# PEER's routing steps spread over the rows of experts up to row 63, with seven tenths of the weights' second parts on GpSimd meanwhile

## The chip, the cores and the metric

One core of a Trainium2 chip runs the whole program. The metric is device microseconds of one execution. The kernel before took 2245.97, 2244.51 and 2240.70 us in three runs: the median is 2244.51.

## The reference

Two blocks run one after the other on 256 tokens of width 1024 (16 meta tokens ahead of them). The first block has a mixer (a state-space model beside a convolution) and a PEER layer; the second has two layers of attention between SwiGLU layers. The change is in PEER. Cut to what matters, in float32:

```
q  = x @ w_query                      # 256 tokens, 8 heads, two halves of 128
s1 = q1 . sub_keys_1 ; s2 = q2 . sub_keys_2        # 128 scores each
v1, i1 = top_k(s1, 16) ; v2, i2 = top_k(s2, 16)
cand = v1[:, None] + v2[None, :]                   # 16 x 16 per head
top_s, pos = top_k(cand, 16)
expert = i1 * 128 + i2 at pos ; gate = softmax(top_s)
y = sum over the chosen experts of gate * gelu(x . w_down[expert]) * w_up[expert]
```

There are 16384 experts (128 x 128), and each token uses 128 of them (16 in each of 8 heads).

## The kernel before, in words

**All experts are computed.** The kernel does not gather. It multiplies all tokens with all experts' down weights, row by row: a row is 128 experts (the first index fixed), and there are 128 rows. The GELU of a row's 128 x 256 products goes to `buf[:, row]`. A dense map of gates (expert by token, zero for experts that are not chosen) is then multiplied into it, and a second pass over all rows (the up projection, line 999) sums the results over experts in four PSUM banks.

**Weights in two parts.** A float32 product is made of three matmuls of the type fp32r: first part x first part, first x second, second x first. SyncE loads weights in chunks of eight tiles (512 KB, three buffers); `_split` (line 283) turns half a chunk (four tiles) into a first part wH on ScalarE (line 288) and a second part wL = weight - wH (line 294). The second part is made by VectorE or GpSimd: `self.turn` grows by `self.share` for each half chunk, and where it reaches 1, GpSimd takes this one. `wtile` (line 299) keeps up to four half chunks split ahead. A row of experts has eight weight tiles: 24 matmuls of 256 columns, and two second parts. `self.share` is 0.7 in the query stage (left from the mixer), 0.5 in the rows and 0.0 from the up projection on.

**The stages of `peer` (line 796).** First the queries (line 845): 16 tiles of q, each evacuated by VectorE to `buf[:, 100 + m % 4]` (lines 834, 835), multiplied with the keys (rows 104 to 111) one tile later (line 840), and the scores copied to rows 112 to 127 (line 841). Then the 128 rows of the down projection (loop at line 964). While they run, VectorE does the routing in two generators, `route(0)` and `route(1)` (line 869), one for each half of the tokens. A route has 40 steps: 16 top-16 lists over 128 scores (lines 863 to 867: MAX8, FIND_INDEX8, MATCH_REPLACE8, MAX8, FIND_INDEX8), sums of candidates (line 881), eight lists over 54 candidates, for eight heads an equality with an iota, a product and a reduction over 16 x 54 elements (lines 894, 895, 897), a softmax with its Exp on ScalarE (line 901), index arithmetic (lines 909 to 914), and three PE transposes with copies to `sel` and `gsel` (lines 918 to 922). The loop takes 1.5 steps after each row.

**Where the routing's scratch lies.** The scratch is in rows of `buf` that are not yet written: `hot` (16 x 54 per head) in rows 72 to 98, `small` from row 60 on. `carve` cuts `small` into v (256 values, one row), ii (one row), fi (one row), cand, cidx and smaller ones, some eight rows in all. The tile framework finds which instructions touch the same bytes and makes the later one wait.

**Gates.** From row 60 on (line 975) each row brings one group of four tokens: `onehot` (line 928) makes one-hot vectors of the two halves of the index on VectorE (line 931) and scales one by the gates (line 933, or line 936 on ScalarE); one row later `gates` (line 938) multiplies them on PE (line 943) to the 128 x 128 gate map of each token, VectorE multiplies it into the rows that are done (line 945), and ScalarE copies the rest into the rows that are to come (line 947). For those `value` (line 954) multiplies GELU and gates (lines 957 to 961), on GpSimd in odd rows. The first gates stand at row 61, the last (of 64) at row 124. After row 127, `act` (line 988) splits `buf[:, 0]` for the up projection.

**Order.** The framework lays out the order of each engine's queue when the program is built, by the source's order and by what is ready; the engines then run their queues in order.

```
    at += n                                   # carve: small[:, at : at + n]
    v = carve(8, 2, 16)
    ii = carve(8, 2, 16)
    q = buf[:, 100 + m % 4]                   # qf
```

Of the kernel before, what the change touches and what calls it, by code (L numbers as in the profile page):

```python
# [21 lines left out]
S = 256  # L22
# [185 lines left out]
class Net:  # L208
# [587 lines left out]
    def peer(self):  # L796
# [4 lines left out]
        NT = P  # L801
        with ExitStack() as ctx:
# [6 lines left out]
            rows = lambda a, b: buf[:, a:b].rearrange("p a b -> p (a b)")  # L809
# [1 line left out]
            keys = rows(104, 112).rearrange("p (h w k) -> p h w k", w=2, k=P)  # L811
            nc.scalar.dma_start(out=keys, in_=self.I["keys"])
            hot = rows(72, 99)[:, : 128 * 54].rearrange("p (h j c) -> p h j c", j=16, c=54)
            small = rows(60, 72)
            at = 0

            def carve(*shape):
# [110 lines left out]
            def onehot(g):  # L928
                o = oh[g % 2]
                ts = slice(4 * g, 4 * g + 4)  # L930
                nc.vector.tensor_tensor(out=o, in0=self.iota[:, None, None, :].to_broadcast([P, 4, 2, P]), in1=sel[:, ts, :, None].to_broadcast([P, 4, 2, P]), op=ALU.is_equal)  # L931
                if g % 4 == 0:
                    nc.vector.tensor_tensor(out=o[:, :, 0], in0=o[:, :, 0], in1=gsel[:, ts, None].to_broadcast([P, 4, P]), op=ALU.mult)
                else:
                    for t in range(4):
                        nc.scalar.activation(out=o[:, t, 0], in_=o[:, t, 0], func=AF.Copy, scale=gsel[:, 4 * g + t : 4 * g + t + 1])  # L936

            def gates(g, R):

                o = oh[g % 2]  # L940
                ps = self.bank("acc").rearrange("p (i t) -> p i t", t=4)
                for t in range(4):
                    nc.tensor.matmul(ps[:, :, t], o[:, t, 1], o[:, t, 0], start=True, stop=True)  # L943
                ts = slice(4 * g, 4 * g + 4)
                nc.vector.tensor_tensor(out=buf[:, :R, ts], in0=ps[:, :R], in1=buf[:, :R, ts], op=ALU.mult)
                if R < NT:
                    nc.scalar.activation(out=buf[:, R:, ts], in_=ps[:, R:], func=AF.Copy)

            pace = 0.0
            work = [x for tt in range(2) for x in [route(tt)]]  # L950
# [3 lines left out]
            def value(r, ps):  # L954
                n = 4 * done
                if n < S:
                    nc.scalar.activation(out=buf[:, r, n:], in_=ps[:, n:], func=AF.Gelu)
                if n:
                    t = self.t_("t", 2)
                    nc.scalar.activation(out=t[:, :n], in_=ps[:, :n], func=AF.Gelu)  # L960
                    (nc.gpsimd if r % 2 else nc.vector).tensor_tensor(out=buf[:, r, :n], in0=t[:, :n], in1=buf[:, r, :n], op=ALU.mult)

            self.share = 0.5
            for r_ in range(NT):
                self.linear(1, KD, self.u(M, T), S, lambda m, ps: value(r_, ps))
                pace += 1.5
                while pace >= 1:
                    pace -= 1
                    while work:
                        try:  # L970
                            next(work[0])
                            break
                        except StopIteration:
                            work.pop(0)
                if r_ >= 60:
                    assert not work
                    if pend >= 0 and done < S // 4:
                        gates(pend, r_ + 1)
                        done += 1
                    if pend + 1 < S // 4:  # L980
                        pend += 1
                        onehot(pend)
# [604 lines left out]
```

## Time and profile before

| | |
|---|---|
| median of three runs | 2244.51 us (2240.70 to 2245.97) |
| the profiled execution's own time | 2239.97 us |
| its span in the profile | 2238.0 us |
| busy: TensorE, VectorE, ScalarE, GpSimd | 2169.0, 1590.4, 1323.0, 671.7 us |
| mean granted TensorE clock | 0.995 |
| second parts on VectorE and on GpSimd (line 294) | 1037 of 731 ns, 259 of 1485 ns |

Times in the views are microseconds from the start of the span, or nanoseconds where marked. In a window view each engine has its busy time and, in brackets, its number of instructions; in a timeline a line has start, length, engine, source line, operation, output and inputs, a count where several stand together, and in square brackets the idle time before it and who ended it. PE is TensorE's matmuls, PEld its weight loads, DVE VectorE, ACT ScalarE, POOL GpSimd, SP SyncE. Matmuls overlap in the records (each shows 280 ns, one begins every 118), so their rate is read from counts.

### The profile page before, as it was taken

The page shows a single profiled execution, that of the slowest core. Times are in us where ns is not written, and L with a number is a line of the kernel's source. Part 1 is how long each engine was busy: PE and PEld are TensorE (multiplying, and loading weights), DVE is VectorE, ACT ScalarE, POOL GpSimd, SP SyncE. Part 2 cuts the span into 40 slices and gives each one's busy share as a digit, 9 for nine tenths or more (in the row PEclk, how much of TensorE's full clock was granted, in tenths as well). Part 3 has the DMA queues.
Part 4 walks back from the last instruction along what each step waited for, and adds up shares of the span by engine and source line. Part 5 has one row for each costly group of instructions (what it writes and reads, how often), then busy time and mean ns, then how long its engine had stood idle before and what let it go on. Part 6 is the DMA issues. An engine that isn't in the chain of part 4 may idle for free.

```text
span 2238.0 us, 45779 instructions
## 1 busy us (share of the span) xinstructions
PE 2169.0 (97%) x17351; PEld 2096.4 (94%) x17351; DVE 1590.4 (71%) x3143; ACT 1323.0 (59%) x2857; POOL 671.7 (30%) x567
## 2 busy tenths in 40 slices
PE   8998998899999999999999999999999999899999
PEld 7987998899999999999999998899999999679999
DVE  8889789955778766666586655876656666877664
ACT  8776654556766755555565555765555555666553
POOL 6684744444555400000031114122201211512220
PEclk9999999999999999999999999999999999999999
DMA  4523644454444555555565554145555555204555
GB/s 170 166 97 133 201 148 142 154 186 151 142 136 139 181 189 188 186 184 188 186 207 188 179 168 144 58 150 173 178 179 170 177 174 187 76 29 128 192 183 169
DMA packets 103948, 356.59 MB, mean 159 GB/s; under 512 B 12416, under 2 KB 20016, under 8 KB 103344
## 3 DMA queue, kind: packets, MB, share of 16 engines
q1 hardware_dynamic: 100096, 346.06, 46.8%
q10 hardware_dynamic: 3632, 7.62, 1.1%
q8 instruction: 136, 2.23, 0.4%
q14 instruction: 84, 0.69, 0.1%
HBM read 351.51 MB, written 5.40 MB: 159 GB/s over the span
## 4 chain that ended last, share of the span: by engine, by line
PE 76%; DVE 14%; ACT 5%; issue 3%; POOL 1%; DMA 1%; DVEq 0%; SPq 0%; ACTq 0%; POOLq 0%
PE acc L999 16%; PE mm L317 13%; PE mm L315 13%; PE mm L316 13%; PE acc L317 4%; PE acc L315 4%; PE acc L316 4%; DVE wL L294 3%; DVE h L931 2%; ACT h L936 1%; ACT wH L288 1%; DVE acc L526 1%; PE mm L1461 1%; PE acc L1485 1%; PE acc L943 1%
## 5 line engine op out<-in xcount | busy, mean ns | idle before, releaser
L288 ACT ACTIVATE wH<-raw 128x512 fp32r<-128x512 f32 x1296 | 806.6, 628 | 559.9 <-PE mm L316 237.8
L294 DVE TENSOR_TENSOR wL<-raw,wH 128x512 fp32r<-128x512 f32 x1037 | 756.3, 731 | 381.0 <-ACT wH L288 358.7
L317 PE MATMUL mm<-uH,wL 128*128 128x256 f32 (+1 forms) x2168 | 620.1, 286 | 19.9 <-DVE wL L294 19.2
L315 PE MATMUL mm<-uH,wH 128*128 128x256 f32 (+1 forms) x2168 | 628.3, 290 | 9.9 <-ACT wH L288 7.0
L316 PE MATMUL mm<-uL,wH 128*128 128x256 f32 (+1 forms) x2168 | 618.9, 286 | 2.4 <-DVE uL L359 2.3
L294 POOL TENSOR_TENSOR wL<-raw,wH 128x512 fp32r<-128x512 f32 x259 | 383.4, 1485 | 462.9 <-ACT wH L288 354.0
L317 PEld LDWEIGHTS mm<-uH,wL 128*128 128x128 f32 x2168 | 411.0, 190 | 24.7 <-DVE wL L294 23.8
L315 PEld LDWEIGHTS mm<-uH,wH 128*128 128x128 f32 x2168 | 410.9, 190 | 15.5 <-ACT wH L288 8.7
L316 PEld LDWEIGHTS mm<-uL,wH 128*128 128x128 f32 x2168 | 410.7, 189 | 5.9 <-DVE uL L359 4.2
L999 PE MATMUL acc<-uH,wH 128*128 128x256 f32 x1024 | 288.4, 282 | 1.7 <-DVE h L1033 1.1
L999 PE MATMUL acc<-uL,wH 128*128 128x256 f32 x1024 | 287.7, 281 | 0.4 <-DVE uL L357 0.4
L999 PE MATMUL acc<-uH,wL 128*128 128x256 f32 x1024 | 287.2, 281 | 0.0
L1086 POOL TENSOR_TENSOR t<-t,g 128x272 f32<-128x272 f32 (+1 forms) x88 | 108.2, 1231 | 415.6 <-ACT wH L288 326.2
L317 PE MATMUL acc<-uH,wL 128*128 128x272 f32 (+1 forms) x728 | 209.4, 288 | 0.0
L315 PE MATMUL acc<-uH,wH 128*128 128x272 f32 (+1 forms) x728 | 209.1, 287 | 0.0
L316 PE MATMUL acc<-uL,wH 128*128 128x272 f32 (+1 forms) x728 | 208.7, 287 | 0.0
L317 PE MATMUL mm<-gH,wL 128*128 128x272 f32 (+1 forms) x704 | 199.9, 284 | 0.0
L315 PE MATMUL mm<-gH,wH 128*128 128x272 f32 (+1 forms) x704 | 199.9, 284 | 0.0
L316 PE MATMUL mm<-gL,wH 128*128 128x272 f32 (+1 forms) x704 | 199.8, 284 | 0.0
L999 PEld LDWEIGHTS acc<-uH,wH 128*128 128x128 f32 x1024 | 194.1, 190 | 2.5 <-DVE h L1033 1.5
L999 PEld LDWEIGHTS acc<-uL,wH 128*128 128x128 f32 x1024 | 193.1, 189 | 0.6 <-DVE uL L357 0.6
L999 PEld LDWEIGHTS acc<-uH,wL 128*128 128x128 f32 x1024 | 193.0, 189 | 0.0
(400 smaller groups left out, 3918.0 us busy)
## 6 DMA issues: line engine op xcount, KB each, us to landing
raw<-in_wall_dram SPq DMA_DIRECT2D x648, 512.0 KB, 3.3
bdram<-brow ACTq DMA_DIRECT2D x1, 3200.0 KB, 13.7
b<-bdram SPq DMA_DIRECT2D x8, 272.0 KB, 4.6
b<-bdram SPq DMA_DIRECT2D x8, 144.0 KB, 4.2
buf<-in_keys_dram ACTq DMA_DIRECT2D x1, 1024.0 KB, 6.4
hd<-h ACTq DMA_DIRECT2D x1, 1024.0 KB, 5.4
h<-hd ACTq DMA_DIRECT2D x1, 1024.0 KB, 6.4
uv<-in_uv_dram ACTq DMA_DIRECT2D x1, 1024.0 KB, 5.8
```

The source lines that it names most:

```text
L288: nc.scalar.activation(out=H, in_=w, func=AF.Copy)
L294: eng.tensor_tensor(out=L, in0=w, in1=H.bitcast(F32), op=ALU.subtract)
L315: mm(ps, H, xH, start=(k == 0), stop=False)
L316: mm(ps, H, xL, start=False, stop=False)
L317: mm(ps, L, xH, start=False, stop=(k == kt - 1))
L526: nc.vector.scalar_tensor_tensor(out=acc, in0=src, scalar=w, in1=acc, op0=ALU.mult, op1=ALU.add)
L931: nc.vector.tensor_tensor(out=o, in0=self.iota[:, None, None, :].to_broadcast([P, 4, 2, P]), in1=sel[:, ts, :, None].to_broadcast([P, 4, 2 ...
L936: nc.scalar.activation(out=o[:, t, 0], in_=o[:, t, 0], func=AF.Copy, scale=gsel[:, 4 * g + t : 4 * g + t + 1])
L943: nc.tensor.matmul(ps[:, :, t], o[:, t, 1], o[:, t, 0], start=True, stop=True)
L999: nc.tensor.matmul(o, a, b, start=(r == 0 and d % 2 == 0 and i == 0), stop=(r == NT - 1 and i == 2), skip_group_check=True)
L1086: nc.gpsimd.tensor_tensor(out=t, in0=t, in1=s, op=ALU.mult)
L1461: nc.tensor.matmul(ps[:, :nk], qa[hh][:, k, a : a + n], ckv[:, k, :nk], start=(k == 0), stop=(k == 1))
```

## The change

The scratch `small` moves from rows 60 to 71 to rows 99 to 110. The gates begin at row 63 (128 - 64 - 1) instead of 60, so that the last of the 64 groups stands at row 127. The routing takes 80 / 62 = 1.29 steps a row instead of 1.5, and is spread over the rows up to the gates. While there is routing left, `self.share` is 0.7 instead of 0.5.

```diff
-            small = rows(60, 72)
+            small = rows(99, 111)
...
-            self.share = 0.5
+            first = NT - S // 4 - 1
             for r_ in range(NT):
+                self.share = 0.7 if work else 0.5
                 self.linear(1, KD, self.u(M, T), S, lambda m, ps: value(r_, ps))
-                pace += 1.5
+                pace += 80 / (first - 1)
                 while pace >= 1:
                     pace -= 1
                     while work:
...
-                if r_ >= 60:
+                if r_ >= first:
                     assert not work
                     if pend >= 0 and done < S // 4:
                         gates(pend, r_ + 1)
```

## Rows read from the trace of the kernel before

**Rows 1.** The page, part 1: busy time, share of the span and instructions.

```profile
PE 2169.0 (97%) x17351; PEld 2096.4 (94%) x17351; DVE 1590.4 (71%) x3143; ACT 1323.0 (59%) x2857; POOL 671.7 (30%) x567
```

**Rows 2.** Windows: length, PE, PEld, DVE, ACT, POOL busy, clock, DMA share, GB/s.

```profile
316.35:374.60 58.25, 51.62 (x401) 50.39 (x402) 58.18 (x147) 29.63 (x57) 24.19 (x16) 0.94 0.42 140
374.60:403.10 28.50, 22.45 (x177) 21.04 (x176) 28.36 (x138) 10.87 (x22) 8.98 (x7) 1.00 0.42 140
411.90:463.90 52.00, 46.47 (x383) 45.25 (x382) 52.00 (x116) 26.89 (x55) 28.30 (x16) 1.00 0.47 154
463.90:516.60 52.70, 52.70 (x449) 52.70 (x448) 15.40 (x24) 27.97 (x55) 24.19 (x19) 1.00 0.60 195
516.60:762.60 246.00, 245.73 (x2097) 244.84 (x2095) 184.33 (x238) 165.42 (x511) 129.00 (x98) 1.00 0.44 144
```

**Rows 3.** Timeline of DVE where routing is done, one such line per row.

```profile
503.08 0.69 DVE L294 TENSOR_TENSOR wL<-raw,wH 128x512 fp32r<-128x512 f32 x1 [2.15 <-ACT wH L288]
```

**Rows 4.** Waits from 318 to 500: us in total, times, longest.

```profile
PE mm L317 <- DVE wL L294: 17.7, 18, 3.0
```

**Rows 5.** Timeline of DVE, where single routing steps run.

```profile
301.72 0.28 DVE L863 MAX8 buf<-buf 128x8 f32<-128x128 f32 x1
...
320.09 0.21 DVE L881 TENSOR_TENSOR buf<-buf 128x64 f32<-128x64 f32 x1
...
374.51 0.22 DVE L914 CAST buf<-buf 128x128 f32<-128x128 int32 x1
...
409.83 0.47 DVE L881 TENSOR_TENSOR buf<-buf 128x128 f32<-128x128 f32 x1 [1.10 <-PE ax L919]
```

**Rows 6.** Timelines of DVE and POOL, the same operations beside GpSimd and alone.

```profile
338.27 2.13 DVE L895 TENSOR_TENSOR buf<-buf 128x864 f32<-128x864 f32 x1
342.97 1.04 DVE L895 TENSOR_TENSOR buf<-buf 128x864 f32<-128x864 f32 x1
358.00 1.04 DVE L897 TENSOR_REDUCE buf<-buf 128x16 f32<-128x864 f32 x1
375.05 1.71 DVE L294 TENSOR_TENSOR wL<-raw,wH 128x512 fp32r<-128x512 f32 x1
358.11 1.30 POOL L294 TENSOR_TENSOR wL<-raw,wH 128x512 fp32r<-128x512 f32 x1 [1.54 <-ACT wH L288]
```

**Rows 7.** Timeline of PE: q tile 12 times the keys (fourth from last).

```profile
303.60 0.61 PE L840 MATMUL ax<-buf 128*128 128x128 f32 x4
```

**Rows 8.** Windows of line 294 alone: length, DVE and POOL busy.

```profile
316.35:374.60 58.25, 13.55 (x15) 24.19 (x16) 0.94 0.42 140
374.60:403.10 28.50, 9.41 (x7) 8.98 (x7) 1.00 0.42 140
411.90:463.90 52.00, 13.38 (x14) 28.30 (x16) 1.00 0.47 154
```

**Rows 9.** Groups by line: busy us, mean ns of one, idle before.

```profile
L895 DVE TENSOR_TENSOR buf<-buf 128x864 f32<-128x864 f32 x16 | 22.3, 1404 | 0.0
L894 DVE TENSOR_TENSOR buf<-buf,cst 128x864 f32<-128x864 f32 x16 | 21.1, 1339 | 0.0
```

**Rows 10.** Chain (first line) and timelines: gates, and the start of line 999.

```profile
516.65 0.89 PE acc L943 x8
517.89 0.41 DVE L945 TENSOR_TENSOR buf<-acc,buf 128x248 f32<-128x248 f32 x1
756.83 0.66 DVE L945 TENSOR_TENSOR buf<-acc,buf 128x500 f32<-128x500 f32 x1
762.94 1.02 ACT L355 ACTIVATE uH<-buf 128x256 fp32r<-128x256 f32 x3
763.40 0.39 PE L999 MATMUL acc<-uH,wH 128*128 128x256 f32 x1 [0.60 <-ACT uH L355]
```

**Rows 11.** Timeline of PE, and a window soon after.

```profile
342.14 0.58 PE L317 MATMUL mm<-uH,wL 128*128 128x256 f32 x1 [2.98 <-DVE wL L294]
...
344.00:346.00 2.00, 2.00 (x11) 2.00 (x11) 2.00 (x4) 0.63 (x1) 0.83 (x1) 0.50 0.58 172
```

## The prediction, on record before the change was run

> **What bounds the kernel now.** The page comes first: TensorE (PE) is busy 97% of the span [rows 1], so only places where it waits can give time. The windows over PEER's down projection come second. From 463.9 to 516.6 us PE runs through [rows 2], and one row of experts (24 matmuls) takes 0.69 + 2.15 = 2.84 us: VectorE (DVE) makes one second part (wL) per row and waits for the next [rows 3]. Before that the reader is to see VectorE full, 58.18 of 58.25, 28.36 of 28.50 and 52.00 of 52.00 us, and PE doing too few matmuls [rows 2]. In the first stretch (S1, 316.35 to 403.10, 86.75 us) it does 401 + 177 = 578, which is 24.1 rows or 68.4 us: 18.4 us lost. In the second (S2, 411.90 to 463.90, 52.0 us) 383, 16.0 rows or 45.3 us: 6.7 us lost. These 25.1 us (1.1%) are all that a better spread can win here; from 516.6 on PE is at work for 245.73 of 246.00 us [rows 2]. The list of waits says for whom PE waits: wL tiles from VectorE, 17.7 us in 18 times, and up to 3.0 [rows 4].
>
> Why is VectorE full, when the source spreads 80 steps over 54 rows? Because the source's spread does not set the order on the queue. The casts that end route 0's index work (L914) belong to its 39th step, row 25 at 1.5 steps a row; they run at 374.51 us, after 401 matmuls or 16.7 rows. Its sums of candidates (L881, steps 17 and 18, row 11) run at 320.09, in row 1, and the twelfth of its 16 top-16 lists, source row 7, begins at 301.72, still in the query stage ahead of every row [rows 2, 5]. The order is laid out when the program is built, and a step goes wherever VectorE would be free. Only PE's transposes keep their source row: VectorE waits 1.10 us for them at 409.83, at row 26 [rows 5]. The real VectorE is slower than that layout allows, mainly through GpSimd: a product of L895 takes 2.13 us where another takes 1.04, and a wL 1.71 where another takes 0.69, while the reduction of L897 keeps its 1.04 with a GpSimd subtraction beginning inside it [rows 3, 6].
>
> **The change, part by part.** The sum is made against the profiled execution: span 2238.0, own time 2239.97; the median of the runs, 2244.51, lies 4.5 us above it.
>
> *Lists pushed out of the query stage (small moves from row 60 to row 99).* The indices (ii) then lie in row 100, which is also q's buffer for every fourth query tile. Every index search must therefore wait until tile 12 of q has been read, by the matmuls at 303.60 [rows 7]. The first MAX8 of each list still fits (v is row 99, free); the other four operations of twelve lists move behind 304 us. The window 374.60 to 403.10 holds route 1's 16 lists and 7 wL: 28.50 - 9.41 = 19.1 us, 1.19 a list [rows 2, 8]. Without its first MAX8 (0.28 [rows 5]) 0.91 remains: 10.9 us for twelve. In the query stage they cost nothing, since VectorE had gaps there; now that cover is gone and they come into S1.
>
> *Seven tenths on GpSimd for 63 rows.* A row has two wL; VectorE's share falls from 1.0 to 0.6, GpSimd's rises from 1.0 to 1.4. What VectorE saves, 0.69 each, the layout fills again with routing: a row then has room for 2.84 - 0.6 x 0.69 = 2.43 us of it, where it had 53.2 / 24.1 = 2.21 (below).
> S1 before: 22 wL took 22.96 us, 15.2 by 0.69 each and 7.8 of blocking; routing took the other 63.8 [rows 8]. The layout's room for that routing was 68.4 - 15.2 = 53.2 us. The moved lists need 0.84 of their real time (16 lists: 177 matmuls or 20.9 us, less 7 x 0.69, is 16.1 for 19.1): 9.2. So S1 after holds (53.2 + 9.2) / 2.43 = 25.7 rows, 73.0 us of PE. VectorE's real work in it: 63.8 + 10.9, then 15.4 wL x (0.69 + 0.35 of blocking) = 16.0, then more blocking of the routing: L894 and L895 average 1.34 and 1.40 over 16 each, 10.6 us above 1.04, half of it in S1 or 0.23 for each of 23 GpSimd subtractions; there will be 36.0, so +3.0 [rows 8, 9]. Sum 93.7, loss 20.7 against 18.4: **+2.3**.
> S2 the same way: 14 wL took 13.38 us (9.7 and 3.7 of blocking), routing 38.6, room 35.6. After: 14.65 rows (41.6 us of PE), and 38.6 + 8.8 x 0.95 + 4.5 x 0.33 = 48.5. Loss 6.9 against 6.7: **+0.2**.
> The trace of before cannot show how tightly the new order is packed, nor how far blocking grows. Lower end: packing stays at 2.21 and the routing is blocked no more. S1 then holds 28.2 rows (80.2) for 92.3 us, 12.1 lost, and S2 47.7 for 45.3, 2.4 lost: together -10.6. Upper end: each added subtraction blocks for its whole 1.30 us [rows 6]: +13.9 and +4.4 on top. I take the middle, since a subtraction blocked 0.57 us in all in S1 ((7.8 + 5.3) / 23) and 0.56 in S2, nearer to the low end than to 1.30.
>
> The rule that bears on this is in the Trainium skill, "SBUF — State Buffer", section "Who interferes with whom": GpSimd and a VectorE operation with two SBUF inputs exclude each other, and the later one stands still for the other's whole instruction. The rows above agree (2.13 against 1.04; the reduction untouched). It speaks against the change: by that rule alone each second part that is moved can cost its full length, the upper end just given.
>
> *Slower pace, 1.5 to 1.29 steps a row.* It moves what follows the source row: route 0's transposes from row 26 to 30, route 1's from 53 to 61. S1 after ends near row 26, so VectorE waits some rows for them where it waited 1.10 us; PE runs meanwhile, and route 1's rest then has rows 31 to 45: 0. No DMA is moved; SP's loads stand as before, and GpSimd has only its subtractions in these rows.
>
> *Gates from row 63.* The same 64 gates, three rows later. Their last product now stands behind row 127, and the up projection's first operand waits for it. Before, PE idled 0.60 us at that change [rows 10]. After: the product begins 1.24 us after the first of its eight gate matmuls (516.65 to 517.89), which take 0.89 of that and only moved; it takes 0.66, and PE goes on 0.46 after the operand's cast begins (762.94 to 763.40) [rows 10]. 0.35 + 0.66 + 0.46 = 1.5 idle: **+0.9**. Ends: 0 if the layout fills it; 2.5 if VectorE comes a row's product late or ScalarE issues its two loads of h, which wait for the last gates, ahead of the cast.
>
> Sum: 2.3 + 0.2 + 0.9 = +3.4, so 2243.4 for the profiled execution and **2247.9** for the median.
>
> **The rivals.**
> A, *the spread works* (faster): the order follows 1.29 steps a row and VectorE has room; S1 and S2 lose only some 4 us: -20, 2224. For it: 102 us of routing, 11 of lists and 38 wL x 0.69 fit into 62 rows (176 us). Against: steps run 8 to 10 rows ahead of the source [rows 5], and a slower source holds back only the transposes.
> B, *relief*: the lower end, -10.6 + 0.9: 2235 to 2240. For it: in the lists' window 7 wL on VectorE took 9.41 us, each held up by GpSimd at the same moment [rows 8], and fewer are left to be held up. Against: freed time is filled with routing.
> C, *the lock* (slower): from +9 up to 3.4 + 18.3, 2254 to 2266. Its place is S1's product stretch (335 to 375 us), and it decides once a subtraction on GpSimd blocks VectorE for over 0.9 us on average. Lateness feeds itself there: PE stood 2.98 us at 342.14, and from 344 to 346 its granted clock was 0.50, the lower of its two levels (1.2 of 2.4 GHz) [rows 11]. The rule of "SBUF — State Buffer" in the Trainium skill, taken alone, means this case.
> D, the change does not do what it says: the pace does not set the order. That is part of the forecast.
>
> **How the numbers follow.** Forecast (-3 to +8) 0.60, A 0.12, B 0.12, C 0.16. Likeliest 2247.9, its own range 2241.5 to 2252.5. For 8 in 10 the range takes in most of B and C's lower part, 2236 to 2258; A, the tip of B and the top of C stay out. No change is within 0.2% (4.5 us), about what a measurement of this kernel can tell. Faster: A and most of B, 0.21. Same: three fifths of the forecast and a little of B, 0.38. Slower: the rest and C, 0.41.
>
> **What would show it.** Right: no index search (L864) before about 303 us; S1 begins with lists and is longer; some 38 wL on VectorE in 63 rows, products still at 2.1 us when GpSimd runs; PE waits for VectorE's wL about as long as before; 1.5 us of idle PE before the first L999. Wrong: lists in the query stage; route 1's products after row 46, or gaps on VectorE in the first 25 rows while PE runs through (A); S1 losing under 14 us (B) or over 27 (C).

## The result, and the profile after

The changed kernel takes 2261.42 us (median of four runs, 2260.17 to 2266.61), the kernel before in the same series 2242.61: ratio 1.0086, 95% interval [1.0067, 1.0105]. That is 19 us slower, and 3.4 us above the upper end of the predicted range. Its profiled execution has a span of 2258.6 us (own time 2260.83), 20.6 more than that of before. In the changed kernel's code the lines behind the change are one higher (L999 is L1000).

The page of the kernel after, its head and the row that answers to [rows 1]:

```profile
span 2258.6 us, 45792 instructions
PE 2180.7 (97%) x17351; PEld 2106.6 (93%) x17351; DVE 1573.0 (70%) x3116; ACT 1324.3 (59%) x2856; POOL 704.2 (31%) x591
```

VectorE (DVE) has 17 us less work, GpSimd (POOL) 32 more, as the change says; TensorE (PE) does the same matmuls and is longer about them. So the time went to places where PE waits or runs slowly. Four events that both traces have place it: the first gates' matmul, the first matmul of the up projection, its last, and VectorE's first addition in the first attention's output projection, with the end of the span.

```
                   gates from   up from   up to    projection from   span
before                 516.5     763.4   1130.2        1469.8       2238.0
after                  530.7     772.8   1140.2        1485.6       2258.6
```

By the end of the up projection 10.0 us are lost; between there and the first attention's projection, 339.6 us of before have become 345.4: another 5.8; behind it another 4.8. **Half of the loss lies in the two attentions, some 560 to 1300 us behind the last row of experts**, where the lines of the diff end (the first runs from about 1340 us on, the second to 2068).

*In PEER.* Windows of the kernel after (length, PE, PEld, DVE, ACT, POOL busy, clock, DMA share, GB/s), to be laid beside [rows 2]:

```profile
316.40:403.00 86.60, 73.69 (x574) 71.24 (x573) 86.50 (x325) 39.16 (x76) 51.93 (x34) 0.96 0.43 141
403.00:426.00 23.00, 20.39 (x173) 20.18 (x172) 8.14 (x23) 10.91 (x22) 13.19 (x11) 1.00 0.55 182
426.00:436.00 10.00, 10.00 (x87) 10.00 (x86) 10.00 (x73) 5.74 (x12) 7.17 (x6) 1.00 0.49 159
436.00:476.00 40.00, 33.27 (x260) 32.46 (x259) 40.00 (x45) 16.77 (x33) 27.08 (x15) 0.95 0.39 132
476.00:530.70 54.70, 54.70 (x454) 54.70 (x453) 13.29 (x16) 30.31 (x62) 33.56 (x26) 0.97 0.58 188
...
316.35:410.00 93.65, 78.12 (x609) 75.47 (x608) 92.55 (x344) 41.49 (x82) 54.94 (x36) 0.96 0.42 136
```

The five windows hold 1548 matmuls, 64.5 rows or 183.1 us at 2.84 a row; they last 214.3 us, so 31.2 us are lost where before lost 25.1: +6.1. (The last line spans the whole work of S1, which ends at 410 us here.) In the first window PE does 574 matmuls, as before in the same 86.6 us (575): VectorE is just as full although GpSimd has 34 second parts there instead of 23, because it now does 325 instructions instead of 284. The rest of S1 runs until 410 us; up to there PE does 609 matmuls, 25.4 rows, and 21.6 us are lost. From 410 to 426 VectorE has only second parts to make, as it waits for route 0's transposes at row 30, and PE runs through. In the second product stretch, 436 to 476, 9.2 us are lost (6.7 in S2 before), and 1.0 behind it. The products of that half, before (412 to 464) and then after (410 to 476):

```profile
L895 DVE TENSOR_TENSOR buf<-buf 128x864 f32<-128x864 f32 x8 | 11.7, 1476 | 0.0
L894 DVE TENSOR_TENSOR buf<-buf,cst 128x864 f32<-128x864 f32 x8 | 9.6, 1218 | 0.0
```

```profile
L895 DVE TENSOR_TENSOR buf<-buf 128x864 f32<-128x864 f32 x8 | 12.1, 1512 | 0.0
L894 DVE TENSOR_TENSOR buf<-buf,cst 128x864 f32<-128x864 f32 x8 | 11.7, 1476 | 0.0
```

*At the change to the up projection.* Timelines of the kernel after, of ACT, DVE and PE, and a window:

```profile
769.77 0.63 ACT L288 ACTIVATE wH<-raw 128x512 fp32r<-128x512 f32 x1
...
770.31 0.61 ACT L288 ACTIVATE wH<-raw 128x512 fp32r<-128x512 f32 x1
770.83 0.15 ACT L957 ACTIVATE buf<-mm 128x4 f32<-128x4 f32 x1
770.88 0.37 ACT L960 ACTIVATE t<-mm 128x252 f32<-128x252 f32 x1
772.36 0.42 ACT L355 ACTIVATE uH<-buf 128x256 fp32r<-128x256 f32 x1 [1.11 <-DVE buf L945]
```

```profile
770.43 1.29 DVE L294 TENSOR_TENSOR wL<-raw,wH 128x512 fp32r<-128x512 f32 x2 [0.17 <-ACT wH L288]
771.65 0.68 DVE L945 TENSOR_TENSOR buf<-acc,buf 128x512 f32<-128x512 f32 x1
```

```profile
768.83 1.05 PE L943 MATMUL acc<-h 128*128 128x128 f32 x8
772.83 0.80 PE L1000 MATMUL acc<-uH,wH 128*128 128x256 f32 x2 [2.95 <-ACT uH L355]
```

```profile
772.80:775.80 3.00, 2.97 (x13) 2.97 (x14) 2.77 (x8) 2.31 (x8) 0.00 (x0) 0.50 1.03 367
```

The gates' last matmul ends at 769.9, but the product that needs it (L945) starts at 771.65: the last GELUs (from 770.83) stood behind ScalarE's wH, and L945 behind two wL. PE idles 2.95 us where it idled 0.60 [rows 10], and the window after it has a granted clock of 0.50, the lower of the two levels: 13 matmuls in 3.0 us, where 25 fit at the upper one. That is 2.35 + 1.4 = 3.8 us, and with the 6.1 above 9.9 of PEER's 10.0 us are placed.

*In the first attention.* The same stretch behind the end of the up projection (+320 to +345 us), before and then after:

```profile
1450.20:1475.20 25.00, 23.42 (x180) 21.23 (x180) 20.53 (x51) 20.18 (x49) 5.69 (x5) 1.00 0.26 85
```

```profile
1460.20:1485.20 25.00, 23.05 (x150) 20.06 (x150) 16.85 (x49) 17.64 (x46) 2.68 (x2) 0.86 0.12 43
```

There are 30 matmuls fewer, a granted clock of 0.86, and of the second parts in this stretch GpSimd makes 2 instead of 3. No line of the attentions was changed. What differs is which second parts GpSimd has there. `_split` adds `self.share` to `self.turn` for every half chunk and gives GpSimd the half at which the sum reaches 1; after PEER's rows a remainder is left, the up projection and the feed-forward layers have share 0 and keep it, and the attentions go on from it at 0.33. By the code it is 0.8 in the kernel before and 1.0 (0.99999) after. Both then give GpSimd the first half and every third, until the sum of 0.33s has slipped by one place: behind the 37th half before, behind the 97th after, of 64 and 46 in the two attentions.

### The profile page after: what moved, and what is told of

The parts are those of the page before. It is cut to its first block, busy times and chain, and to the rows that moved or that the text cites. A ratio compares the mean times of both kernels' runs of the same rounds, so it can differ in the third digit from the quotient of the medians.

```text
span 2258.6 us, 45792 instructions
## 1 busy us (share of the span) xinstructions
PE 2180.7 (97%) x17351; PEld 2106.6 (93%) x17351; DVE 1573.0 (70%) x3116; ACT 1324.3 (59%) x2856; POOL 704.2 (31%) x591
## 4 chain that ended last, share of the span: by engine, by line
PE 80%; DVE 13%; ACT 3%; issue 3%; POOL 1%; DMA 1%; SPq 0%; DVEq 0%; ACTq 0%; POOLq 0%
PE acc L1000 16%; PE mm L317 15%; PE mm L315 15%; PE mm L316 15%; PE acc L315 4%; PE acc L317 4%; PE acc L316 4%; DVE wL L294 2%; PE acc L943 2%; DVE acc L526 1%; PE mm L1462 1%; PE acc L1486 1%; DVE h L931 1%; DVE buf L895 1%; ACT wH L288 1%
## 5 line engine op out<-in xcount | busy, mean ns | idle before, releaser
L294 DVE TENSOR_TENSOR wL<-raw,wH 128x512 fp32r<-128x512 f32 x1012 | 731.4, 724 | 389.0 <-ACT wH L288 371.6
L317 PE MATMUL mm<-uH,wL 128*128 128x256 f32 (+1 forms) x2168 | 622.5, 287 | 21.1 <-DVE wL L294 19.3
L294 POOL TENSOR_TENSOR wL<-raw,wH 128x512 fp32r<-128x512 f32 x284 | 413.2, 1462 | 437.5 <-ACT wH L288 388.2
L1000 PE MATMUL acc<-uH,wH 128*128 128x256 f32 x1024 | 288.9, 282 | 4.0 <-ACT uH L355 2.9
L1000 PE MATMUL acc<-uL,wH 128*128 128x256 f32 x1024 | 288.2, 281 | 0.0
L1000 PE MATMUL acc<-uH,wL 128*128 128x256 f32 x1024 | 287.7, 281 | 0.0
L1000 PEld LDWEIGHTS acc<-uH,wH 128*128 128x128 f32 x1024 | 194.7, 190 | 4.8 <-ACT uH L355 3.1
L1000 PEld LDWEIGHTS acc<-uL,wH 128*128 128x128 f32 x1024 | 193.7, 189 | 0.0
L1000 PEld LDWEIGHTS acc<-uH,wL 128*128 128x128 f32 x1024 | 193.7, 189 | 0.0
```

Of the source, the lines that this page charges most:

```text
L294: eng.tensor_tensor(out=L, in0=w, in1=H.bitcast(F32), op=ALU.subtract)
L317: mm(ps, L, xH, start=False, stop=(k == kt - 1))
L1000: nc.tensor.matmul(o, a, b, start=(r == 0 and d % 2 == 0 and i == 0), stop=(r == NT - 1 and i == 2), skip_group_check=True)
```

## The experiments

Two theories for the attentions: **the remainder** does it, whatever else was changed; or what is late at the end of PEER pushes later work out of step. For PEER four suspects: the moved lists, the larger share, the slower pace, the late gates. The runs of each group stood beside runs of the kernel before on the same chip, whose medians were 2240 to 2243 us; a ratio is taken from all runs of both and is not just the quotient of the two medians. All ratios:

```
kernel                                             median us   ratio to before
after                                               2261.42   1.0086 [1.0067, 1.0105]
e1   after, remainder 0.8                           2252.38   1.0044 [1.0028, 1.0061]
e2   before, remainder 1.0                          2250.72   1.0041 [1.0028, 1.0053]
e11  before, remainder 0.5                          2245.67   1.0013 [1.0005, 1.0022]
e12  before, remainder 0.2                          2249.94   1.0028 [1.0017, 1.0039]
e4   before, lists moved                            2244.03   1.0016 [1.0006, 1.0026]
e5   before, 0.7                                    2250.54   1.0042 [1.0028, 1.0057]
e9   before, 0.7, order in the gates' rows kept     2238.42   0.9985 [0.9974, 0.9996]
e14  before, 0.9, order kept                        2246.54   1.0029 [1.0019, 1.0040]
slower pace, remainder 0.8:  lists   share  gates from row
e3                           moved   0.5    63      2245.71   1.0024 [1.0014, 1.0034]
e7                           query   0.5    63      2243.68   1.0016 [1.0007, 1.0026]
e6                           query   0.7    63      2244.36   1.0021 [1.0012, 1.0031]
e8                           moved   0.7    60      2249.09   1.0040 [1.0023, 1.0057]
e10                          query   0.5    60      2240.75   0.9996 [0.9985, 1.0006]
e13                          query   0.7    60      2237.65   0.9988 [0.9979, 0.9997]
e15                          moved   0.5    60      2241.78   1.0003 [0.9995, 1.0012]
```

**The remainder (e1, e2, e11, e12).** One line more, at the end of the rows; e1 in the kernel after, the others in the kernel before (0.99999, 0.5, 0.2):

```diff
             self.share = 0.0
+            self.turn = 0.7999999999999943
```

> The changed kernel, with self.turn set back after PEER's rows to the value that the kernel before has there (0.8 instead of 1.0). Theory P: half of the loss is not in PEER. The seven tenths leave another remainder in self.turn, and with it other half chunks of the two attention layers go to GpSimd; from there come 5.7 us in the first attention and 4.8 in the second (their stages ended 15.8 and 20.6 us late, where PEER ended 10.1 late). Then this runs at 2261.4 - 10.5 = 2251, attention as in the kernel before, PEER still about 10 us late. Rival Q: attention is late for another reason, such as loads or an order that PEER's later end shifts; then this stays at 2261 (2258 to 2264).

> The kernel before, with self.turn set after PEER's rows to the remainder that the changed kernel leaves (just under 1.0). Theory P: PEER as before, both attention layers as in the changed kernel, 2242.6 + 10.5 = 2253. Rival Q: nothing changes, 2243 (2240 to 2245).

The stretch of the first attention in e1, and then in e2:

```profile
1462.20:1487.20 25.00, 23.42 (x179) 21.24 (x180) 20.43 (x55) 20.96 (x55) 4.34 (x4) 1.00 0.25 73
```

```profile
1452.00:1477.00 25.00, 23.05 (x150) 20.06 (x150) 16.84 (x49) 17.67 (x46) 2.67 (x2) 0.86 0.13 43
```

The kernel after with the old remainder has the stretch of before (179 matmuls, clock 1.00), and the kernel before with the new remainder has that of after, to the last matmul. The remainder alone costs 0.0041 to 0.0042, some 9 us, whatever happened in PEER; the theory of late work falls, since e2's PEER is the old one. Both came out as theory P said.

> The kernel before, with 0.5 in the counter at the end of the rows instead of 0.8: in the attentions GpSimd's every third half lies one place later than in the kernel before up to its 36th half, at the same places to the 52nd, and one later from there on. Theory N (what costs in the kernel after is GpSimd on the halves number 0, 3, 6 of each three, past the 36th): within 3 us of before, ratio 0.999 to 1.001. Rival L (any change of the pattern from the one before costs 5 to 10 us): ratio 1.002 to 1.005. Rival G (the pattern before is not the best either): ratio under 0.999.

> The kernel before, with 0.2 in the counter at the end of the rows: GpSimd's halves lie two places later up to the 36th, one later to the 61st, and from there on at the places that they have in the kernel after. Theory N: the first attention as before, the second about 4 us longer, ratio 1.001 to 1.003. Rival L: ratio 1.003 to 1.006. Rival G: under 0.999.

Neither is as good as 0.8. e11 lies above theory N's range; e12 lies in it, but not in the way that N said: its first attention (end of the up projection to the first addition, 1129.3 to 1476.2) takes 346.9 us, not the 339.6 of before. So N's simple rule, one bad place of three, falls: the places of before are the best of four that ran, and which rule makes them so stays open, as does the wait in the attentions through which a place costs time.

**The parts alone, at the old pace (e4, e5, e9, e14).**

```diff
-            small = rows(60, 72)            # e4
+            small = rows(99, 111)
...
-            self.share = 0.5                # e5; and 0.8 left at the end
             for r_ in range(NT):
+                self.share = 0.7 if work else 0.5
```

> The kernel before with the scratch alone moved from row 60 to row 99. Theory: no index search before 303 us, some 11 us of lists come into VectorE's full stretch, and PEER ends 2 to 5 us later: 2245 to 2248. Rival, the moved lists cost nothing because the later wait for route 0's transposes takes them up: 2242.6 within 1 us. Rival, they cost their whole length: 2253.

> The kernel before with the seven tenths alone (as long as routing steps are left; self.turn set back to 0.8 behind the rows; scratch, pace and gates as before). Theory, blocking takes back what VectorE saves: the products L894 and L895 average 1.47 and 1.69 us as in the changed kernel (1.34 and 1.40 before), PEER ends 3 to 8 us late, 2243 to 2248 beside 2240. Rival, relief: the lists stay in the query stage and VectorE has a tenth less to do, so this is 4 to 10 us faster, 2230 to 2236. Rival, the seven tenths hurt only together with the moved lists: 2240 within 2 us.

The lists cost 0.0016 alone, 3.6 us, as e4's theory said. The share cost 0.0042, more than any of e5's theories said, and where it lost them was not expected. e5's profiled execution (the slowest of its five, 2258.54) was some 6 us late ahead of the rows, in stages that no edit touches: the last score matmul (line 840) begins at 320.0 us, before at 313.9. From there to the first gates it takes 197.7 us, before 202.6: the larger share gains 4.9 us there. But the rows behind the first gates, whose share is one half in both kernels, take 249.0 us instead of 237.5. The groups of line 294 there (560 to 760 us), before and then in e5, and two lines of e5's timelines:

```profile
L294 DVE TENSOR_TENSOR wL<-raw,wH 128x512 fp32r<-128x512 f32 x53 | 42.1, 795 | 7.8 <-ACT wH L288 6.4 <-ACT buf L947 0.7 <-POOL buf L961 0.6
```

```profile
L294 DVE TENSOR_TENSOR wL<-raw,wH 128x512 fp32r<-128x512 f32 x50 | 60.0, 1201 | 0.0
```

```profile
599.36 1.77 DVE L294 TENSOR_TENSOR wL<-raw,wH 128x512 fp32r<-128x512 f32 x1
```

```profile
598.22 2.36 POOL L294 TENSOR_TENSOR wL<-raw,wH 128x512 fp32r<-128x512 f32 x1 [1.10 <-ACT wH L288]
```

It is the counter again. During each row two half chunks (of a later row) are split; at one half, started from 0.8, GpSimd gets the first of the two and VectorE the second. In e5 the seven tenths left another remainder at the change of share, and the order is turned round: VectorE's now begins inside GpSimd's (599.36 inside 598.22 to 600.58) and takes 1201 ns on average, not 795. (In the kernel after the order is that of before, as the share changes at row 63 instead of 54.) e9 keeps the order (and has seven tenths for six rows more):

```diff
+                self.share = 0.7 if r_ < 60 else 0.5
+                if r_ == 60:
+                    self.turn = 0.7999999999999943
```

> The kernel before, with seven tenths up to row 60 at the old pace, the counter set at row 60 so that in the gates' rows GpSimd again takes the first half of each row and VectorE the second (as before; with the counter run through, as in the earlier run with the share alone, VectorE had the first half, and its subtractions took 1201 ns instead of 795), and 0.8 left at the end of the rows. Theory R (the loss of the run with the share alone was the flipped order in the gates' rows): gates 237.5 us long again, span and time within 3 us of before, ratio 0.999 to 1.002. Rival Q (the share itself slows the routing's products by holding VectorE off the port): the gates begin 2 to 6 us later than before and all of it reaches the end, ratio 1.002 to 1.004. Rival B (the relief helps): ratio under 0.999.

0.9985, with an interval that ends just below 1: the relief is real, though small, and e5's loss came with the turned order and not with the share. PE's waits from 316 to 517 us in e9, beside 17.7 in 18 times before [rows 4]:

```profile
PE mm L317 <- DVE wL L294: 14.0, 10, 2.4
PE mm L317 <- POOL wL L294: 0.5, 1, 0.5
```

This is theory B's result, which the prediction gave 0.12. e14 is the same with 0.9:

> The kernel before, with nine tenths in place of one half up to row 60, the order in the gates' rows and the remainder kept. With seven tenths so, the ratio was 0.9985 and PE waited 14.0 us instead of 17.7 for VectorE's second parts. Theory B (each further half taken off VectorE gives as much): ratio 0.996 to 0.998. Rival G (GpSimd becomes the bound: 1.8 halves a row at 1.5 us are 2.7 of the row's 2.84, so that PE waits for GpSimd's): ratio 1.000 to 1.004, and over 8 us of waits for GpSimd's wL.

Waits (316 to 530) and groups (316 to 517) of e14:

```profile
PE mm L317 <- DVE wL L294: 13.9, 4, 4.9
PE mm L317 <- POOL wL L294: 5.0, 10, 1.9
```

```profile
L895 DVE TENSOR_TENSOR buf<-buf 128x864 f32<-128x864 f32 x16 | 30.4, 1935 | 0.0
L294 DVE TENSOR_TENSOR wL<-raw,wH 128x512 fp32r<-128x512 f32 x14 | 12.8, 912 | 56.4 <-ACT wH L288 56.4
```

Rival G's ratio, with less of its wait (5.0 of the 8 named): VectorE makes only 14 of the second parts, but its 16 products take 1935 ns on average (1404 before [rows 9]), and each late one holds PE up to 4.9 us. So of one half, seven tenths and nine tenths the middle one is best at the old pace.

**The parts beside the slower pace (e3, e6, e7, e8, e10, e13, e15).** All have 80 units over the rows up to the gates and 0.8 left at the end. They differ in three edits to the kernel after: the lists in the query stage again, with all scratch in rows that are free; the gates from row 60; the share one half (e10 has all three, e3 only the last; e8 and e15 leave out the first, e7 the second; e6 has the first alone; e13 has the first two, with e9's lines in place of the third):

```diff
-            hot = rows(72, 99)[:, : 128 * 54].rearrange("p (h j c) -> p h j c", j=16, c=54)
+            hot = rows(84, 111)[:, : 128 * 54].rearrange("p (h j c) -> p h j c", j=16, c=54)
-            small = rows(99, 111)
+            small = rows(72, 84)
...
-            first = NT - S // 4 - 1
+            first = 60
...
-                self.share = 0.7 if work else 0.5
+                self.share = 0.5
```

> The changed kernel with the share left at one half in all rows: scratch moved, slower pace, gates from row 63, but no more work for GpSimd; the remainder of self.turn is then that of the kernel before. Theory: attention as before; PEER keeps the lists that were pushed out of the query stage and the idle time before the up projection (about 4 us) and loses the added blocking, so PEER is 4 to 9 us late, 2247 to 2252. Rival, the lock is all of PEER's loss: only the idle time is left, 2246 or 2247. Rival, the seven tenths help and the spread hurts: PEER over 10 us late, above 2253.

> The changed kernel with self.turn set back and the scratch laid where no query tile lies (small in rows 72 to 83, the one-hot scratch behind it): lists can run in the query stage again. Theory: index searches begin near 270 us, the 4 us of the moved lists come back, 2252.4 - 4 = 2248. Rival, the moved lists are no part of the loss once GpSimd has seven tenths: 2252. Rival, they are most of it: under 2244.

> The changed kernel with the same free scratch and the share at one half: only the slower pace and the later gates are left. Theory: the pace does nothing and the last gates cost 1.5 to 2.5 us ahead of the up projection, so 2241.5 to 2243 beside 2240. Rival A, the spread works by itself: routing steps run later than before and the result is faster, under 2236. Rival: the wait ahead of the up projection is as long as in the changed kernel (3 us idle, then half the clock), 2244 or more.

> The changed kernel with self.turn set back and the gates at row 60 again (steps 80/59 = 1.36 a row). Theory: the idle time ahead of the up projection falls from 2.95 us to that of the kernel before (0.6) and the clock does not fall there: 3 to 4 us less than 2252.4, so 2248 to 2249.5. Rival, the wait was hidden anyway: 2252 within 1 us.

None of the four came out clearly: e3, at 2245.7, is faster than its theory's 2247 to 2252 and nearest to its first rival, e6 lies between its theory and its last rival, e7 is just above its theory's 2243, and e8, inside its 2248 to 2249.5 by the time, is by the ratio only 0.0004 better than e1. With the gates at row 63 the share made no difference that can be told apart (e6 to e7), and the lists little at one half (e3 to e7, 0.0008). The corners with the gates at 60 were still missing:

> The kernel after with its share put back to one half, the short lists and the products in rows that are free from the first one, and the gates from row 60 again at 80 units in 59 rows: the slower pace alone. Theory T (what was left at that free scratch and half share, ratio 1.0016, was the late gates: the last group of gates falls on row 127, and the wait for it costs 3 us and a stretch at half clock): the up projection starts 0.6 us after the last uH and before 763, ratio 0.999 to 1.0005. Rival D (the slower pace itself costs, as the routing's results now come just before the gates): the gates start over 2 us later than before, ratio 1.001 to 1.003. Rival S (the spread helps once the gates aren't late): ratio under 0.999.

> The run with the slower pace alone (gates from row 60, 80 units in 59 rows, lists and products in free rows), with seven tenths up to row 60, the first half of each gates row on GpSimd and 0.8 left at the end. Theory A (the share's gain of 0.0015 at the old pace adds to the slower pace's 0.9996): ratio 0.997 to 0.999, gates from 510 to 513. Rival H (the slower pace already spreads the queue on VectorE, so that the relief finds nothing): ratio 0.999 to 1.001, gates from 515 to 519. Rival K (GpSimd's longer use of the port slows the products of the spread routing): ratio 1.001 to 1.003.

> The kernel after at half share and with the gates from row 60 again (80 units in 59 rows): the slower pace and the moved lists. It fills the fourth corner beside the lists in the query stage at one half (0.9996) and at seven tenths (0.9988), and the moved lists at seven tenths (1.0040). Theory L (the lists' own time, which came to 3.7 us in the prediction's way of counting, whatever the share): ratio 1.001 to 1.0025, so that 2 to 6 us of the 1.0040 belong to both together. Rival M (they cost 9 us or more at the slower pace, whatever the share): 1.003 to 1.006. Rival Z (they cost nothing without the larger share): 0.999 to 1.0005.

e10 has the slower pace and other free rows for the scratch, nothing else, and its time is that of before: theory T's ratio, the pace itself costs and gives nothing. (T's sign "before 763" failed in e10's profiled execution, 766.1 after 1.33 us of idle PE; it was 1.5 us late ahead of the rows.) Late gates are what e7 has more, 0.0020, and e6 over e13, 0.0033; between e1 and e8 it is 0.0004, whose uncertainty (0.002) doesn't exclude the others. (The profiled executions of e10 and e13 are the slowest of their 12 and 11, at 2245.84 and 2243.88; the ratios are from all.) e13 adds the share: 0.9988, theory A's ratio, though so near to H's that the interval takes in both. Its gates begin at 516.2, which looks like H's, but its last score matmul comes at 319.5, 5.6 us later than before; from there the gates come 5.9 us sooner than before, as A said. Against the kernel before its interval is just below 1: it is the second version that beats both kernels, e9 the first. The four corners at row 60 then say what the lists cost: 0.0007 at one half (e15 over e10, theory Z), but **0.0052 at seven tenths** (e8 over e13), which alone gains 0.0008. With the gates at row 63, the place that they have in the kernel after, the same two costs are 0.0008 (e3 over e7) and 0.0023 (e1 over e6), and by their intervals these two can't be told apart. The traces say more. From the last scores to the first gates, in us, one execution each (three rows more are 8.5; before, e2, e11 and e12, which are the same up to there, take 201.9 to 204.3, and the kernel after takes 216.6, as e1 does):

```
                                   lists in the query stage   moved
gates from row 60, share one half        203.0 (e10)       203.0 (e15)
gates from row 60, seven tenths          196.7 (e13)       207.6 (e8)
gates from row 63, share one half        211.7 (e7)        210.3 (e3)
gates from row 63, seven tenths          206.2 (e6)        216.7 (e1)
```

At one half the moved lists cost nothing here (0.0 and -1.4; at the old pace e4 takes 205.5, 2.9 more than before), at seven tenths 10.9 and 10.5; the share gains 5.5 to 6.3 with the lists in the query stage and loses 4.6 to 6.4 with the lists moved. Each edit is nearly harmless without the other.

One stretch in which that can be seen is 355 to 380 us. The kernel after: groups, timelines of DVE and of POOL, and the window:

```profile
L294 POOL TENSOR_TENSOR wL<-raw,wH 128x512 fp32r<-128x512 f32 x9 | 16.8, 1881 | 9.0 <-ACT wH L288 8.8
L895 DVE TENSOR_TENSOR buf<-buf 128x864 f32<-128x864 f32 x6 | 11.6, 1957 | 0.0
L894 DVE TENSOR_TENSOR buf<-buf,cst 128x864 f32<-128x864 f32 x4 | 6.2, 1590 | 0.0
L897 DVE TENSOR_REDUCE buf<-buf 128x16 f32<-128x864 f32 x6 | 6.2, 1041 | 0.0
L294 DVE TENSOR_TENSOR wL<-raw,wH 128x512 fp32r<-128x512 f32 x4 | 3.9, 981 | 0.0
```

```profile
361.96 4.19 DVE L894 TENSOR_TENSOR buf<-buf,cst 128x864 f32<-128x864 f32 x2
366.07 4.21 DVE L895 TENSOR_TENSOR buf<-buf 128x864 f32<-128x864 f32 x2
```

```profile
361.57 7.81 POOL L294 TENSOR_TENSOR wL<-raw,wH 128x512 fp32r<-128x512 f32 x4 [2.97 <-ACT wH L288]
```

```profile
355.00:380.00 25.00, 20.16 (x140) 19.55 (x140) 25.00 (x21) 8.88 (x18) 16.03 (x9) 0.86 0.39 119
```

Groups and window of e13:

```profile
L895 DVE TENSOR_TENSOR buf<-buf 128x864 f32<-128x864 f32 x4 | 5.2, 1303 | 0.0
L894 DVE TENSOR_TENSOR buf<-buf,cst 128x864 f32<-128x864 f32 x3 | 4.2, 1409 | 0.0
L294 DVE TENSOR_TENSOR wL<-raw,wH 128x512 fp32r<-128x512 f32 x4 | 3.9, 984 | 0.0
```

```profile
355.00:380.00 25.00, 21.57 (x171) 20.36 (x171) 25.00 (x71) 9.30 (x19) 14.04 (x9) 1.00 0.43 148
```

And of e15:

```profile
L895 DVE TENSOR_TENSOR buf<-buf 128x864 f32<-128x864 f32 x6 | 7.9, 1323 | 0.0
L894 DVE TENSOR_TENSOR buf<-buf,cst 128x864 f32<-128x864 f32 x5 | 5.4, 1074 | 0.0
```

```profile
355.00:380.00 25.00, 22.78 (x191) 22.37 (x190) 25.00 (x26) 11.48 (x23) 11.36 (x8) 1.00 0.45 149
```

In the kernel after four products come without a pause from 361.96 to 370.28, and beside them four of GpSimd's subtractions without a pause from 361.57 to 369.38: each product takes 2.1 us. PE does 140 matmuls at a granted clock of 0.86, where e13 does 171 and e15 191, both at 1.00. Both of those also pass through products here (e13's end at 367.8), beside 9 and 8 subtractions, and L895 stays at 1.3; the reductions (L897) take their 1.04 everywhere. In e8, the corner itself, PE does 137 matmuls in this window at 0.87, in e1 137 at 0.86. That lining up of products and subtractions in long trains is what the trace shows of the two edits together; why the layout puts them so wasn't tried. It is also only a part of the 10.9 us: over all 32 products, the time above 1.04 us is 15.3 us in e8 (means 1496 and 1539 ns) and 12.2 in e13 (1502 and 1342), 3 us more. The lists' own time on VectorE and the lower clock stand beside it; how the other 8 us divide between them isn't shown.

## Why the prediction was wrong

**The counter (a term that was missing).** This is the step that put the time outside the range. The sum stopped at the up projection and put nothing for what stands behind it. That the remainder of the counter is carried on, into the attentions, could be read in `_split`; it is 9 of the 19 us (e2: 0.0041). With the old remainder the change would have cost 10 us: 2252.4 (e1), within the range and at the upper end of the forecast's own. Taking the edits back one by one gives 0.0042 for the counter (after to e1), 0.0028 for lists and share (e1 to e7), 0.0020 for the late gates (e7 to e10) and -0.0004 for the pace.

**The lists and the share (the sum right in S1, by luck in part).** S1 was to hold 25.7 rows in 93.7 us and to lose 20.7; it holds 25.4 in 93.65 and loses 21.6. (The loss before was 18.7 rather than 18.4: the 578 matmuls count three on the border of two windows twice.) But the two parts of it were far off in opposite ways. Without the moved lists the prediction's way of counting has 53.2 / 2.43 = 21.9 rows in S1, 62.2 us, for 63.8 + 13.1 x 1.04 + 7.6 x 0.23 = 79.2: 17.0 lost, 1.4 less than before, and with S2's +0.2 a gain of 1.2 for the share. The lists are then 20.7 - 17.0 = 3.7. By the ratios the share alone gave 3.4 (e9) and 1.8 (e13 over e10), by the traces up to the first gates (195.8 in e9 for 202.6) 6.8 and 6.3. The lists alone cost 3.6 (e4) and 1.6 (e15), but 11.7 beside the larger share (e8 over e13). Together the prediction said +2.5; the kernel after's trace has +6.1 by the five windows, e1 over e7 is 0.0028 or 6 us, e8 over e10 0.0044 or 10. The step that failed here is the mean price of blocking, "0.23 for each subtraction" for the products, taken as the same whatever stands beside what. In 355 to 380 it was (6 x 0.92 + 4 x 0.55) / 9 = 0.86 us for each of the nine (products above 1.04), in e13 0.24. With VectorE's own second parts (above 0.69) it is 0.99 and 0.37. That is rival C's mechanism with its own condition (over 0.9), but in one stretch of 25 us. Over S1 up to 403 us it is 0.41 in the kernel after (9.9 us on products and 4.1 on 13 second parts, for 34 subtractions), where the forecast's terms come to 13.7 / 36 = 0.38. So C's 2254 to 2266 held the result only because the counter added 9 us.

The Trainium skill's "SBUF — State Buffer", section "Who interferes with whom", has the later of the two stand still for the other's whole instruction. The train agrees (2.1 us where 1.04 is the length alone); but that each moved second part costs so much, as that rule alone would have it, e9 excludes: 24 more halves on GpSimd, and 3.4 us less.

**S2 (mis-sized).** Predicted +0.2; 9.2 us were lost for 6.7 before, and 1.0 more behind it. The sixteen products there took 7.3 us more than 1.04 each would, before 4.9: 2.4 more, where the forecast added 1.5 for all blocking of the routing. And the granted clock, 1.00 in S2 before [rows 2], was 0.95 over 436 to 476 and 0.50 from 476 to 478.

**The tail (mis-sized).** Predicted +0.9, at most 2.5; it was 3.8 in the trace, and the late gates are 0.0020 between e7 and e10. The product's place behind row 127 was right. The queues ahead of it were left out: three wH on ScalarE, two wL on VectorE, and then 1.4 us at the lower clock.

**The pace.** "The pace does not set the order" was right: e10 is 0.9996. Route 0's transposes moved to row 30 as forecast, and PE ran through meanwhile.

**What was to be seen, in turn.** No index search before 303 us: the first is at 302.70, when tile 12's matmuls end in this execution. Some 38 wL on VectorE: 39 by 530.7 us. S1 begins with lists: yes, 325 instructions on VectorE instead of 284 by 403 us. PE waits for wL about as long: 19.3 us in 12 times (17.7 in 18). Idle of 1.5 us at L999: 2.95. Loss of S1 between 14 and 27: 21.6.

## What to carry to other kernels

A fractional counter that hands out work is state: whoever changes its rate in one stage changes the order in every later one, so reset it where a stage begins, and look at which unit each engine gets, not only how many. An edit that costs 0 to 4 us alone can cost 10 beside another that gains by itself, so try the corners and not only each edit alone. A mean price per blocked operation is only good for the order that it was measured in. Before trusting a sum that ends at a stage, compare the stages behind it event by event, and count from an event that the edits leave alone: executions here were up to 6 us apart ahead of the first row.

## What the runs showed of the hardware

The order in which the two subtractions of a row were handed out, to GpSimd first or second, made VectorE's 128 x 512 second part 795 or 1201 ns on average with half of them on each engine either way. And after a pause of 2.95 us with no matmul at 769.9 to 772.8 the granted clock was 0.50 for the next 3.0 us, as it was after the 2.98 us of [rows 11]: here the wait cost about 1.4 us more than itself. The length of the wait alone doesn't tell whether the clock falls. In the kernel after, two waits of the same length in S2 were followed by 1.00 and by 0.50 (timeline of PE and windows):

```profile
462.46 0.38 PE L317 MATMUL mm<-uH,wL 128*128 128x256 f32 x1 [2.06 <-DVE wL L294]
475.01 0.38 PE L317 MATMUL mm<-uH,wL 128*128 128x256 f32 x1 [2.03 <-DVE wL L294]
```

```profile
464.00:468.00 4.00, 3.91 (x34) 3.71 (x33) 4.00 (x5) 2.12 (x5) 1.41 (x1) 1.00 0.62 246
476.00:478.00 2.00, 2.00 (x12) 2.00 (x11) 1.07 (x1) 0.90 (x3) 0.00 (x0) 0.50 0.75 256
```
